# S5's recurrence by fours of tokens instead of pairs, in the first mixer of a two-block model on one Trainium2 core

## The chip, the cores and the metric

One core of one Trainium2 chip runs the kernel. The metric is device time in microseconds (us) of one execution, the median of several runs. A group of rows of the profile is one profiled execution of the same kernel.

## The reference

Two layers of a first block and two of a second run over one sequence of 256 tokens with 1024 channels, in 32-bit floats. Only the mixer of the first layer bears on the change. Half of its projected columns go through RWKV-7, the other half through S5, and a projection back follows:

```python
def s5_ssm(u, lam_re, lam_im, log_dt, b_re, b_im, c_re, c_im, d_skip, w_glu, b_glu):
    ug = u.reshape(b, t, 32, 16)                       # 32 groups of 16 channels
    lam = lax.complex(lam_re, lam_im)                  # 64 states a group
    lam_bar = jnp.exp(lam * jnp.exp(log_dt)[:, None])
    b_bar = ((lam_bar - 1.0) / lam)[..., None] * lax.complex(b_re, b_im)
    bu = jnp.einsum('gpi,btgi->btgp', b_bar, ug)
    # x[t] = lam_bar x[t - 1] + bu[t], an associative scan over the tokens
    y = jnp.real(jnp.einsum('gip,btgp->btgi', c_mat, states)) + d_skip * ug
    y = gelu(y.reshape(b, t, 512))
    return y * sigmoid(y @ w_glu + b_glu)
```

The mixer is `concat(rwkv7(z[..., :1824]), s5_ssm(z[..., 1824:])) @ hy_w_out` with `z = rms_norm(h) @ hy_w_in`, added to h. The layer's next part, attention to a memory of 256 rows, projects `rms_norm(mem)` to keys and values; that work doesn't depend on the mixer.

## The kernel before

Tokens lie along the free dimension and channels on the partitions. Every weight is loaded in tiles of 2048 columns (`weight`, L157) and split into two parts whose products are exact, wh by ScalarE (L177) and wl by VectorE (L180); a product by a weight is three matmuls (`mm3`). The order of the program is the order of priority. A planner puts each engine's instructions into one fixed queue by it, so an instruction that waits holds all behind it on its engine. A tile name with one buffer is handed to its next user, in program order, only when all readers of the tile before are done; the tiles named rw_... belong to RWKV's working memory and are lent to other work in this way. PSUM has four banks acc, two banks ps, and one each for s5_p and s5_py.

`hybrid_mix` (L898) puts the first mixer together. The projections (`hybrid_in`, L390) come first; u, the input of S5, is the last of them, two transposed banks copied by ScalarE. `next(ssm)` runs S5's setup before that. `mem_norm` (L973) loads the two blocks of the memory on SP's queue into rw_XK (one buffer, so the second block waits for the first's readers) and the gain into rw_MB. Then `mix` steps through `rwkv` (L426), which does two halves of 128 tokens with some 39 yields each, and between its yields takes steps of two others at written-out positions: the last projections and S5 in one chain, and `mem_kv`, the memory's projections to keys and values.

```python
at = (2, 5, 7, 9, 13, 20, 27, 34, 41, 45, 55, 61, 64, 75, 77), (21, 28, 35, 39, 49, 56, 65, 73, 76)
kv = mix(self.rwkv(z, y), (chain(proj, ssm), at[0]), (self.within_aside(self.mem_kv(0, mn, "")), at[1]))
```

RWKV bounces its small blocks through DRAM on SP's queue, and uses rw_MB (L538), rw_XK (L540), rw_G (L634) among others in each half. Its result of a half is split into yh and yl (L220).

S5 (`s5`, L718) holds 128 states on the partitions, two groups of channels at once, 16 such pairs (q). It carries the state from an odd token to the next: x[t] = l^2 x[t-2] + l B u[t-1] + B u[t], with the complex state turned back by its own angle so that the scan is real. The setup makes the decay and the angle (also once per input channel), Lt = l B (L784 to L791), the output matrices Cc and CL, and K0 = C B, the direct part of an even token, by 32 products of 32 columns. The loop has two halves j0 of four steps i; a step handles two q of 128 states by 128 pairs of tokens. It computes angles for them (L825 to L828), sine and cosine on ScalarE (`sincos`, L890), the state inputs (8 products of 32 rows, 128 columns), the turn (L839 to L842), four scans of 128 columns (L846), the turn back (L847 on), and the outputs: CL's and Cc's products of 128 columns on 32 output partitions, with the two q beside each other on the array, and K0's. After each half `d u` is added; a Gelu (L867) closes. `s5_glu` (L869) and the product by hy_w_out follow RWKV's end, then the residual (L302).

Of the kernel before, what the change touches and what calls it, by code (L numbers as in the profile page):

```python
# [19 lines left out]
S = 256  # L20
# [62 lines left out]
class Rows:  # L83
    """tiles that hold the 128-row blocks of a matrix, indexed [partitions, block, columns]"""
# [8 lines left out]
class Model:  # L93
# [23 lines left out]
    def phase(self, name, nb=2, nacc=4, nps=0, nx=1):  # L117
        """working memory of one phase"""
# [8 lines left out]
    def weights(self, name, nw, nraw):  # L127
        """buffers of the weights"""
# [6 lines left out]
    def more_raw(self, name, n):  # L135
        """n more buffers of the weights as loaded"""
# [20 lines left out]
    def weight(self, src, a, b, then=None):  # L157
        """src: AP [128, a, b] in DRAM -> (h, l) viewed [128, a, b], in halves of a; then() comes after the first half"""
# [27 lines left out]
    def fetch(self, src, a, b, pool=None):  # L186
        """src as loaded"""
# [5 lines left out]
    def wcols(self, w, c0, c1):  # L193
        """columns c0:c1 of w [K, N], all of K"""
# [3 lines left out]
    def wrows(self, w, k0, k1):  # L198
        """128-row blocks k0:k1 of w [K, N], all of N"""
# [16 lines left out]
    def split(self, h, l, src, scale=None):  # L216
        """src (F32) -> h + l; scale: [P, 1]"""
# [5 lines left out]
    def ntile(self, sh, name, bufs=2, dt=F32, pool=None):  # L223
        """a tile for the norms, which outlives the phases unless it belongs to work on the side"""
# [4 lines left out]
    def rstd(self, ss, n, width, eps, pool=None):  # L229
        """[128, n] sums of squares -> (ss / width + eps) ** -0.5"""  # L230
# [7 lines left out]
    def bcast(self, src, n, queue=None):  # L238
        """row src [n] of DRAM to all partitions"""
# [21 lines left out]
    def row_norm(self, src, g, xn):  # L261
        """a generator: xn = rms_norm of a block times g; returns the last instructions"""
# [8 lines left out]
    def norm_t(self, h, gain, parts=None, pre=None, tg=None):  # L271
        """rms_norm(h) * gain (or pre, its two token blocks), transposed and split: (xh, xl) [128, 8, 256]; parts: split by token too"""
# [29 lines left out]
    def residual(self, h, accs, hold=False):  # L302
        """h += accs (token block, column half)"""
# [45 lines left out]
    def rows_all(self, accs, w, at, order):  # L349
        """accs = at x w, in the order of the row blocks given"""  # L350
# [5 lines left out]
    def lin_t(self, w, c0, x):  # L356
        """256 columns of x @ w, transposed: bank [128, 2, 256] (column block, token)"""
# [25 lines left out]
    def shifted(self, p, f, i, dst, n=128):  # L383
        """token shift of the transposed projection p[:, f]: z + (z[t - 1] - z) * mu"""
# [5 lines left out]
    def hybrid_in(self, h, pool):  # L390
        """a generator: the projections in order of need; then yields for those of the last two"""
# [9 lines left out]
        # a small weight, in room of its own  # L401
# [19 lines left out]
        for j in range(2):  # L421
            p = self.lin_t(w, 1824 + j * 256, x)
            nc.scalar.copy(u[:, 2 * j:2 * j + 2, :], p.rearrange("p (f t) -> p f t", f=2))
            yield

    def rwkv(self, z, ya):  # L426
        """time mix of the shifted projections, a generator; split, transposed result into ya"""
# [25 lines left out]
        def head_sums(x):  # L453
            """sums over the channels of each head of x [128, 4, 128]: bank [:, :8], token on the partitions"""
# [5 lines left out]
        for hf in range(2):  # L460
# [4 lines left out]
            # normalised key  # L465
# [15 lines left out]
            # log decay, in-context learning rate  # L481
# [15 lines left out]
            # decay products from the start of each chunk of 64  # L497
# [9 lines left out]
            # alpha | rho, beta, kappa  # L507
# [12 lines left out]
            # products within chunks: rows s, columns t of alpha | rho  # L520
# [21 lines left out]
            # inverses of the 16 x 16 diagonal blocks, one block per partition  # L542
# [8 lines left out]
            tmp = T("Lt", [64, 64])  # L551
            Dm = DE[:, 0]
            with self.tc.issue_after(self.floor[1].ins):
                nc.vector.tensor_copy(Dm, self.cc("i16")[:64].rearrange("p (t s) -> p t s", t=16))
# [9 lines left out]
            Dc = T("Dc", [128, 2, 8, 16])  # L564
# [10 lines left out]
            # token-major copies  # L575
# [10 lines left out]
            # bonus weights  # L586
# [7 lines left out]
            # gate  # L594
# [8 lines left out]
            def both(lhsT, rhs):  # L603
                """block-diagonal lhsT: both chunks of each head at once"""
# [5 lines left out]
            def pairs(cols, lhsT, rhs):  # L610
                """[64 x 64] products for each head and chunk, chunk on the partitions"""
# [61 lines left out]
            # over the chunks  # L673
# [21 lines left out]
            # norm over each head, bonus, gate  # L695
# [22 lines left out]
    def s5(self, u, pool, brief, ps, yg):  # L718
        """the state is carried from one odd token to the next: x[t] = l^2 x[t - 2] + l B u[t - 1] + B u[t];
        an even token's output is C l x[t - 1] + C B u[t]"""  # L720
        nc, t = self.nc, self.t
        T = lambda name, sh, bufs=1: pool.tile(sh, F32, name="s5_" + name, bufs=bufs)
        V = nc.vector
        H = S // 2
        # per state (its index on the partitions | its group's input on them): decay, angle per token in turns
        N = 272
        par = self.work.tile([128, 1024], F32, name="rw_G", bufs=1)
        nc.scalar.dma_start(par[:, :3 * N], t["s5_par"])
        lr, li, dt = (par[:, e * N:(e + 1) * N] for e in range(3))
        tmp = self.work.tile([128, 1024], F32, name="rw_RW", bufs=1)  # L730
        r, f = tmp[:, :N], tmp[:, N:2 * N]
        m1, m2, q1, q2 = (tmp[:, 2 * N + e * 16:2 * N + (e + 1) * 16] for e in range(4))
        sico = self.work.tile([128, 1024], F32, name="rw_AR", bufs=1)[:, :2 * N].rearrange("p (e n) -> p e n", e=2)
        si, co = sico[:, 0], sico[:, 1]
        keep = T("keep", [128, 3, 16])
        fh, fl, r2 = (keep[:, e] for e in range(3))
# [8 lines left out]
        V.tensor_scalar(fh, f[:, :16], 1536.0, -1536.0, ALU.add, ALU.add)  # L745
        V.tensor_sub(fl, f[:, :16], fh)
        V.tensor_mul(r2, r[:, :16], r[:, :16])
        self.sincos(f, sico, N)
        V.tensor_mul(co, co, r)
        V.tensor_mul(si, si, r)  # L750
        # input coefficient
        a = slice(0, 16)
        lr, li = lr[:, a], li[:, a]
        cm = dt[:, a]
        V.tensor_scalar_add(cm, co[:, a], -1.0)
# [5 lines left out]
        V.tensor_mul(m2, si[:, a], li)  # L761
        V.tensor_add(q1, q1, m2)
        V.tensor_mul(q1, q1, m1)
        V.tensor_mul(q2, si[:, a], lr)
# [3 lines left out]
        # input and output matrices, block-diagonal over pairs of groups  # L768
        C = [T(n, [128, 16, 32], 2) for n in ("w1", "w2")]
        Bs = [self.work.tile([128, 16, 32], F32, name="rw_" + n, bufs=1) for n in ("Kt", "V")]  # L770
        for x, n in zip(C + Bs, ("s5_cT_re", "s5_cT_im", "s5_b_re", "s5_b_im")):
            nc.gpsimd.memset(x, 0.0)
            src = (t[n][0] if n in ("s5_b_re", "s5_b_im") else t[n]).rearrange("(q g) p i -> g p q i", g=2)
            for g in range(2):
                nc.scalar.dma_start(x[g * 64:(g + 1) * 64, :, g * 16:(g + 1) * 16], src[g])
        Bt, Lt = (brief.tile([128, 4, 2, 64], F32, name=n) for n in ("Bt", "Lt"))
        for e, n in enumerate(("re", "im")):
            nc.scalar.dma_start(Bt[:, :, e], t["s5_bT_" + n].rearrange("(j g) i p -> (g i) j p", g=8))

        def times(dst, x, y, cr, ci, sg):  # L780
# [1217 lines left out]
```

## Time and profile before

| | before |
|---|---|
| runs (us) | 2490.81, 2493.50, 2493.89; median 2493.5 |
| span of the profiled execution (us) | 2491.7 |
| its time outside the span | the page gives none |
| TensorE (PE) busy | 2406.4 us, 97% |
| VectorE (DVE) busy | 1863.9 us, 75% |
| ScalarE (ACT) busy | 1542.0 us, 62% |
| GpSimd (POOL) busy | 63.3 us, 3% |

PE is TensorE's matmul, PEld its load of weights. A row of instructions gives the line of the kernel, the engine, the operation, output<-inputs, the tile's shape and the number of instructions (x). In a timeline the first column is the start and the second the duration in us, both from the span's start; what stands in brackets is idle time before the instruction and what ended it. A 4-byte matmul leaves two records, one for each of its passes, but for the types that the split weights have. The granted clock is a share of 2.4 GHz; 0.5 is the lower level, 1.2 GHz. The busy shares are of the whole program; of the part that the change touches only the first mixer's stretches tell.

### The profile page before, as it was taken

To read this page: it belongs to the slowest core of one execution; us is meant where nothing else is said; L and a number is where in the kernel's file an instruction comes from. 1 tells how busy PE (TensorE), PEld (TensorE's weight loads), DVE (VectorE), ACT (ScalarE), POOL (GpSimd) and SP (SyncE) were. 2 spreads that over 40 slices of the span, in tenths; PEclk is the share of its full clock that TensorE was granted. 3 is DMA by queue.
4 is the path that set the end of the run, shared out by engine and by line. 5 is a ranking of instruction groups with operands and counts; after the bars stand their busy time and mean duration, and the time that the engine had idled before them with its cause. 6 is when DMAs were issued, how large, how long until landed. Compare 5 with 4: busy or idle time off the path is not lost. (4 is left out here: it accounts for less than half of the span.)

```text
span 2491.7 us, 37696 instructions
## 1 busy us (share of the span) xinstructions
PE 2406.4 (97%) x14914; PEld 2093.2 (84%) x14914; DVE 1863.9 (75%) x2533; ACT 1542.0 (62%) x2235; POOL 63.3 (3%) x78
## 2 busy tenths in 40 slices
PE   7999999999998999999999999999889999999998
PEld 7888789989887888888888888888778899887998
DVE  7888655556655989898989898989756776665776
ACT  5545554445544877777777777777655555555554
POOL 1000000001100000000000000000000000000000
PEclk9899999999999999999999999999989999998999
DMA  8323555554474989999999999999663455633653
GB/s 241 89 87 126 180 170 186 187 175 138 148 277 149 332 326 345 345 361 363 351 346 362 367 365 340 358 363 352 234 207 113 156 186 186 195 112 102 209 186 106
DMA packets 338764, 586.75 MB, mean 235 GB/s; under 512 B 28620, under 2 KB 173938, under 8 KB 338322
## 3 DMA queue, kind: packets, MB, share of 16 engines
q1 hardware_dynamic: 314752, 557.75, 64.6%
q10 hardware_dynamic: 23826, 26.50, 3.4%
q8 instruction: 119, 1.95, 0.3%
q14 instruction: 67, 0.55, 0.1%
HBM read 578.56 MB, written 6.82 MB: 235 GB/s over the span
## 5 line engine op out<-in xcount | busy, mean ns | idle before, releaser
L180 DVE TENSOR_TENSOR wl<-wraw,wh 128x1024 fp32r<-128x1024 f32 x1054 | 1247.1, 1221 | 349.7 <-ACT wh L177 345.2
L177 ACT CAST wh<-wraw 128x1024 fp32r<-128x1024 f32 x1054 | 1077.5, 1052 | 423.3 <-PE ps L203 254.3
L203 PE MATMUL ps<-wh,xh 128*128 128x512 f32 (+1 forms) x1472 | 458.8, 359 | 1.6 <-DVE xl L220 1.6
L203 PE MATMUL ps<-wl,xh 128*128 128x512 f32 (+1 forms) x1472 | 449.0, 352 | 0.0
L203 PE MATMUL ps<-wh,xl 128*128 128x512 f32 (+1 forms) x1472 | 448.8, 352 | 0.0
L203 PEld LDWEIGHTS ps<-wh,xh 128*128 128x128 f32 x1472 | 252.7, 193 | 40.1 <-issue 2.9
L203 PEld LDWEIGHTS ps<-wh,xl 128*128 128x128 f32 x1472 | 250.7, 192 | 38.8 <-issue 0.7
L203 PEld LDWEIGHTS ps<-wl,xh 128*128 128x128 f32 x1472 | 251.4, 192 | 36.2 <-issue 0.5
L203 PE MATMUL ps<-xh,wh 128*128 128x256 f32 x1424 | 208.2, 286 | 4.4 <-ACT wh L177 1.6
L203 PE MATMUL ps<-xh,wl 128*128 128x256 f32 x1424 | 207.0, 285 | 0.0
L203 PE MATMUL ps<-xl,wh 128*128 128x256 f32 x1424 | 206.0, 284 | 0.0
L203 PEld LDWEIGHTS ps<-xh,wh 128*128 128x128 f32 x1424 | 188.4, 192 | 10.7 <-issue 2.4
L203 PEld LDWEIGHTS ps<-xh,wl 128*128 128x128 f32 x1424 | 186.9, 192 | 1.6 <-issue 1.2
L203 PEld LDWEIGHTS ps<-xl,wh 128*128 128x128 f32 x1424 | 186.5, 192 | 1.2 <-issue 1.2
L203 PE MATMUL acc<-wh,e_ah 128*128 128x512 f32 x448 | 177.1, 395 | 0.1
L203 PE MATMUL acc<-wh,e_al 128*128 128x512 f32 x448 | 175.7, 392 | 0.0
L203 PE MATMUL acc<-wl,e_ah 128*128 128x512 f32 x448 | 175.6, 392 | 0.0
L203 PE MATMUL acc<-wh,ah 128*128 128x512 f32 x264 | 103.3, 391 | 0.0
L203 PE MATMUL acc<-wh,al 128*128 128x512 f32 x264 | 103.3, 392 | 0.0
L203 PE MATMUL acc<-wl,ah 128*128 128x512 f32 x264 | 103.2, 391 | 0.0
L203 PEld LDWEIGHTS acc<-wh,e_al 128*128 128x128 f32 x448 | 83.9, 187 | 20.3 <-DVE e_al L220 0.4
L203 PEld LDWEIGHTS acc<-wh,e_ah 128*128 128x128 f32 x448 | 84.1, 188 | 18.4 <-ACT e_ah L220 0.3
(582 smaller groups left out, 2795.3 us busy)
## 6 DMA issues: line engine op xcount, KB each, us to landing
wraw<-moe_w_up SPq DMA_DIRECT2D x112, 1024.0 KB, 7.3
wraw<-moe_w_gate SPq DMA_DIRECT2D x112, 1024.0 KB, 7.2
wraw<-moe_w_down SPq DMA_DIRECT2D x112, 1024.0 KB, 7.0
wraw<-w_up SPq DMA_DIRECT2D x44, 1024.0 KB, 5.1
wraw<-w_down SPq DMA_DIRECT2D x22, 1024.0 KB, 4.9
wraw<-w_in SPq DMA_DIRECT2D x20, 1024.0 KB, 6.4
wraw<-xa_w_kv SPq DMA_DIRECT2D x16, 1024.0 KB, 5.8
wraw<-da_w_qkv SPq DMA_DIRECT2D x12, 1024.0 KB, 5.1
```

The costliest lines, as they stand in the source:

```text
L177: nc.scalar.copy(h[:, :m], r)
L180: nc.vector.tensor_sub(l[:, :m], r, h.bitcast(F32)[:, :m])
L203: self.nc.tensor.matmul(out, lhsT, rhs, start=start, stop=stop)
```

## The change

S5 carries its state from one fourth token to the next.

- u is copied as [v, m], token 4 m + v, so that each of the four tokens of a four is a block of 64 columns.
- Parameters: 16 columns each in place of 272 (s5_par from 408 to 24 KB); the copy of B by input channel (0.26 MB) and the constants for it are gone, and the constants of the mixer are 448 columns narrower, or 0.23 MB.
- Setup: B l^k and C l^k for k = 0 to 3 come from one chain of seven complex products on VectorE, six operations of 256 columns each. The powers of B lie in rw_XK and rw_RW, those of C in a tile named y, which is RWKV's result later. All angles, 16 x 64, are made at once in rw_MB and rw_MT, and their sines and cosines kept in two tiles of 1024 columns.
- For each i of four, ScalarE spreads the powers into block-diagonal matrices BX (rw_De1) and LX by 4 and 2 copies; 8 products of 128 columns make K, the direct parts by distance 0 to 3; 8 transposes, in two acc banks, make the state input matrices B, copied out by ScalarE.
- The inputs of a four are stacked on the partitions in U (rw_G) by 16 transfers on ScalarE's queue, 32 partitions each.
- Loop: four steps of four q, each 128 states by 4 x 64 columns. The state inputs are 8 products of 128 rows and 64 columns; the scans two of 256 columns, whose decay row R4 GpSimd makes, with zeros where a q begins; the outputs 64 products of 64 columns, with neighbours on four different quarters of the output partitions. The direct terms are 4 products each of 192, 128, 64 columns with K, and of 64 with the skip d on the diagonal. The result of a step replaces its part of U.
- Channels are permuted by that; s5_w_glu, s5_b_glu and hy_w_out are permuted to match on the host, outside the timed kernel, and s5_glu restores the tokens' order as it splits.
- RWKV's unit matrix is made by two fills on GpSimd in place of a copy; two of its small tiles take names of others.
- S5 stands in `mix` by itself, at earlier positions.

```diff
-                nc.scalar.copy(u[:, 2 * j:2 * j + 2, :], p.rearrange("p (f t) -> p f t", f=2))
+            for f in range(2):
+                nc.scalar.copy(u[:, 2 * j + f].rearrange("p (v m) -> p v m", v=4), p[:, f * 256:(f + 1) * 256].rearrange("p (m v) -> p v m", v=4))
...
-            tmp = T("Lt", [64, 64])
+            tmp = T("Lp", [64, 64])
...
-                nc.vector.tensor_copy(Dm, self.cc("i16")[:64].rearrange("p (t s) -> p t s", t=16))
+            nc.gpsimd.memset(Dm, 0.0)
+            nc.gpsimd.memset(Dm.rearrange("p t s -> p (t s)")[:, ::17], 1.0)
...
-            Dc = T("Dc", [128, 2, 8, 16])
+            Dc = T("Lc", [128, 2, 8, 16])
...
+        def times(E, dst, x, y, cr, ci, sg, name):
+            for d, z, w, sub in ((dst[0], x, y, sg > 0), (dst[1], y, x, sg < 0)):
+                c = T(name, [128] + list(x.shape[1:]))
+                E.tensor_tensor(d, z, cr, ALU.mult)
+                E.tensor_tensor(c, w, ci, ALU.mult)
+                E.tensor_tensor(d, d, c, ALU.subtract if sub else ALU.add)
+        BC = [W(n, [128, 4, 16, 16]) for n in ("XK", "RW")]
+        C = [T(n, [128, 16, 16]) for n in ("w1", "w2")]
...
+        LC = pool.tile([128, 2, 4, 16, 16], F32, name="y")
+        times(V, (LC[:, 0, 0], LC[:, 1, 0]), C[0], C[1], b16(q1), b16(q2), 1, "R4")
+        V.tensor_scalar_mul(LC[:, 1, 0], LC[:, 1, 0], -1.0)
+        for k in range(3):
+            times(V, (BC[0][:, k + 1], BC[1][:, k + 1]), BC[0][:, k], BC[1][:, k], b16(ck), b16(sk), 1, "R4")
+            times(V, (LC[:, 0, k + 1], LC[:, 1, k + 1]), LC[:, 0, k], LC[:, 1, k], b16(ck), b16(sk), -1, "R4")
+        LX, BX = brief.tile([128, 4, 2, 4, 32], F32, name="LX"), W("De1", [128, 4, 2, 4, 32])
...
+        sc = self.gp.tile([128, 16 * M], F32, name="gain"), T("sc", [128, 16 * M])
+        y, z = W("MB", [128, 16, M]), W("MT", [128, 16, M])
...
+        self.sincos(y.rearrange("p q m -> p (q m)"), sc)
...
+        for i in range(4):
+            spread(BX, BC, i)
+            spread(LX, LC, i)
+            for j in range(4):
+                for e in range(2):
+                    self.mm(p[32 * i:32 * i + 32, j * 128:(j + 1) * 128], BX[:, j, e, 0, :], LX[:, j, e].rearrange("p d o -> p (d o)"),
+                            e == 0, e == 1)
+            for x in range(2):
+                pt = self.accs(1)[0]
+                for j in range(2):
+                    for e in range(2):
+                        nc.tensor.transpose(pt[:, (2 * j + e) * 128:(2 * j + e + 1) * 128], BX[:, 2 * x + j, e].rearrange("p k o -> p (k o)"), self.ident)
+                nc.scalar.copy(B[:, i, 2 * x:2 * x + 2], pt.rearrange("p (j e n) -> p j e n", j=2, e=2))
...
+            yield
+        U = W("G", [128, 4, 4, M])
+        for i in range(4):
+            for v in range(4):
+                nc.scalar.dma_start(U[32 * (3 - v):32 * (3 - v) + 32, i], u[32 * i:32 * i + 32, :, v * M:(v + 1) * M])
...
+        for i in range(5):
+            if i:
+                h = i - 1
...
+                for v in range(4):
+                    for n, (cx, x) in enumerate(terms):
+                        for j in range(4):
+                            c = (h + j) % 4
+                            o = py[32 * c:32 * c + 32, v]
+                            if v < 3:
+                                self.mm(o[:, 1:], LX[:, j, cx, v + 1, :], x[:, j, :-1], False, False)
+                            else:
+                                self.mm(o, LX[:, j, cx, 0, :], x[:, j], False, n == 3)
+                nc.scalar.copy(U[:, h], py)
...
+            spread(LX, LC, i)
...
+            R4 = T("R4", [128, 4, M])
+            G.tensor_tensor(R4, self.cc("reset")[:, None, :M].to_broadcast([128, 4, M]), r4[:, i::4, None].to_broadcast([128, 4, M]), ALU.mult)
...
+        nc.scalar.activation(yg, U.rearrange("p i v m -> p i (v m)"), AF.Gelu_apprx_tanh)
...
-            at = (2, 5, 7, 9, 13, 20, 27, 34, 41, 45, 55, 61, 64, 75, 77), (21, 28, 35, 39, 49, 56, 65, 73, 76)
-            kv = mix(self.rwkv(z, y), (chain(proj, ssm), at[0]), (self.within_aside(self.mem_kv(0, mn, "")), at[1]))
+            at = (2, 5, 7, 9), (4, 6, 8, 10, 12, 16, 20, 24, 28), (21, 28, 35, 39, 49, 56, 65, 73, 76)
+            kv = mix(self.rwkv(z, y), (proj, at[0]), (ssm, at[1]), (self.within_aside(self.mem_kv(0, mn, "")), at[2]))
```

## Rows read from the trace of the kernel before

**Rows 1.** The page of the kernel before, its first line.
```profile
span 2491.7 us, 37696 instructions
```

**Rows 2.** Windows: stretch, length, busy PE PEld DVE ACT POOL, clock, DMA share, GB/s.
```profile
45.00:85.00 40.00, 36.99 (x394) 35.11 (x395) 37.39 (x77) 28.77 (x48) 2.08 (x1) 1.00 0.57 156
85.00:118.00 33.00, 31.26 (x237) 25.42 (x232) 24.36 (x73) 12.15 (x23) 1.10 (x2) 0.74 0.21 58
118.00:232.00 114.00, 111.86 (x1204) 100.66 (x1204) 98.70 (x244) 58.44 (x103) 6.23 (x6) 1.00 0.30 92
232.00:264.30 32.30, 29.47 (x376) 25.89 (x376) 21.45 (x37) 12.64 (x23) 1.64 (x1) 1.00 0.55 190
```

**Rows 3.** Windows, the stretch from 90 to 107 alone.
```profile
90.00:107.00 17.00, 16.50 (x86) 13.40 (x86) 13.88 (x42) 4.24 (x10) 0.55 (x1) 0.51 0.31 96
```

**Rows 4.** Timeline of PE, one step of the S5 loop, 173 to 181.
```profile
173.08 2.08 PE L203 MATMUL s_p<-zu,s_B 32*128 32x128 f32 x16
175.09 0.39 PE L203 MATMUL ps<-wl,xh 128*128 128x256 f32 x1
...
177.68 1.06 PE L203 MATMUL s_py<-s_w,CL 128*32 128x127 f32 x16
178.57 1.04 PE L203 MATMUL s_py<-s_w,Cc 128*32 128x128 f32 x16
179.54 1.06 PE L203 MATMUL acc<-call,rw_sq 128*128 128x8 f32 x8
180.53 0.42 PE L203 MATMUL s_py<-zu,s_K 32*32 32x128 f32 x4
```

**Rows 5.** Timeline of PE, RWKV's sums of 8 columns and K0's product, 57 to 62.
```profile
57.55 0.95 PE L203 MATMUL acc<-call,rw_sq 128*128 128x8 f32 x8
58.35 0.36 PE L203 MATMUL ps<-xh,wl 128*128 128x256 f32 x1
...
60.67 0.22 PE L203 MATMUL s_p<-Cc,rw_V 128*32 128x32 f32 x1
...
61.43 0.39 PE L203 MATMUL ps<-xh,wl 128*128 128x256 f32 x1
```

**Rows 6.** Timeline of PE, two rows of four transposes, and what follows, 201 to 203.
```profile
201.83 0.66 PE L583 MATMUL acc<-ident,zv 128*128 128x128 f32 x4
...
202.85 0.38 PE L203 MATMUL s_p<-zu,s_B 32*128 32x128 f32 x1
```

**Rows 7.** Groups of VectorE by form, 16 to 278: count | busy us, mean ns | idle.
```profile
L180 DVE TENSOR_TENSOR wl<-wraw,wh 128x1024 fp32r<-128x1024 f32 x44 | 53.3, 1221 | 5.6 <-ACT wh L177 5.6
L846 DVE TENSOR_TENSOR_SCAN s_st<-s_keep,s_w 128x128 f32<-128x128 f32 x32 | 11.6, 404 | 0.0
...
L847 DVE TENSOR_TENSOR s_w<-s_st,s_sc 128x512 f32<-128x512 f32 x8 | 5.5, 684 | 0.0
...
L840 DVE TENSOR_TENSOR s_w<-s_w,s_w 128x256 f32<-128x256 f32 x8 | 3.3, 416 | 0.0
```

**Rows 8.** Timelines of ACT and DVE, places where memory is handed on, 65 to 265.
```profile
65.26 0.68 DVE L791 TENSOR_TENSOR CL<-CL,s_st 128x512 f32<-128x512 f32 x1
...
83.54 0.63 ACT L253 ACTIVATE xl<-rw_XK 128x512 fp32r<-128x512 f32 x1 [1.82 <-PE ps L203]
...
98.20 0.74 DVE L538 TENSOR_TENSOR rw_MB<-acc,call 128x256 f32<-128x256 f32 x2
...
112.80 1.29 DVE L540 TENSOR_TENSOR rw_XK<-acc,call 128x512 f32<-128x512 f32 x2 [4.69 <-PE ps L290]
...
133.79 0.68 DVE L634 TENSOR_TENSOR rw_G<-rw_RW,acc 128x512 f32<-128x512 f32 x1
...
264.50 0.68 DVE L220 TENSOR_TENSOR yl<-rw_ka,yh 128x512 fp32r<-128x512 f32 x1
```

**Rows 9.** Timelines of POOL and of ACT's DMA queue.
```profile
59.38 2.08 POOL L473 TENSOR_TENSOR rw_ks<-rw_ks,mhalf 128x8 f32<-128x8 f32 x1 [42.48 <-DVE rw_ks L472]
...
133.91 0.37 ACTq L996 DMA_DIRECT2D kv<-a_m_kT  x1
```

More of the change, by code (lines that the diff above doesn't have):

```diff
@@ L721, in s5 @@
         nc, t = self.nc, self.t
[L722 to L728, printed above, removed]
-        lr, li, dt = (par[:, e * N:(e + 1) * N] for e in range(3))
[L730 to L736, printed above, removed]
+        T = lambda name, sh: pool.tile(sh, F32, name="s5_" + name)
+        W = lambda name, sh: self.work.tile(sh, F32, name="rw_" + name, bufs=1)
+        V, G = nc.vector, nc.gpsimd
+        M = S // 4
+        N = 16
+        par, tmp = W("G", [128, 3 * N]), W("AR", [128, 6 * N])
+        nc.scalar.dma_start(par, t["s5_par"])
+        lr, li, dt = (par[:, e * N:(e + 1) * N] for e in range(3))
+        r, f, si, co, m1, m2 = (tmp[:, e * N:(e + 1) * N] for e in range(6))
+        keep = T("keep", [128, 7, 16])
+        fh, fl, r4, q1, q2, ck, sk = (keep[:, e] for e in range(7))
         nc.scalar.activation(dt, dt, AF.Exp)
@@ L760, in s5 @@
         V.tensor_mul(q1, cm, lr)
-        V.tensor_mul(m2, si[:, a], li)
+        V.tensor_mul(m2, sk, li)
         V.tensor_add(q1, q1, m2)
         V.tensor_mul(q1, q1, m1)
-        V.tensor_mul(q2, si[:, a], lr)
+        V.tensor_mul(q2, sk, lr)
         V.tensor_mul(m2, cm, li)
@@ L767, in s5 @@
         V.tensor_mul(q2, q2, m1)
[L769 to L775, printed above, removed]
@@ new lines, in s5 @@
+        skip = T("skip", [128, 4, 32])
+        for i in range(4):
+            g = slice(32 * i, 32 * i + 32)
+            V.tensor_tensor(skip[g], self.ident[g, None, g].to_broadcast([32, 4, 32]),
+                            self.pps("s5_d", 4)[g, :, None].to_broadcast([32, 4, 32]), ALU.mult)
+        yield
+        self.sincos(y.rearrange("p q m -> p (q m)"), sc)
+        K = T("K", [128, 4, 4, 32])
+        p = ps.tile([128, 512], F32, name="s5_p")
+        B = brief.tile([128, 4, 4, 2, 128], F32, name="B")
@@ new lines, in s5 @@
+        LC = LC.rearrange("p e k q o -> p (e k) q o")
+        for i in range(4):
[5 more added lines that the diff above has]
+                            e == 0, e == 1)
+            for x in range(2):
+                pt = self.accs(1)[0]
+                for j in range(2):
+                    for e in range(2):
+                        nc.tensor.transpose(pt[:, (2 * j + e) * 128:(2 * j + e + 1) * 128], BX[:, 2 * x + j, e].rearrange("p k o -> p (k o)"), self.ident)
+                nc.scalar.copy(B[:, i, 2 * x:2 * x + 2], pt.rearrange("p (j e n) -> p j e n", j=2, e=2))
+            if i == 3:
+                nc.scalar.copy(K, p.rearrange("p (j d o) -> p j d o", j=4, d=4))
+                V.tensor_tensor(K[:, :, 0], K[:, :, 0], skip, ALU.add)
+            yield
@@ L881, in s5_glu @@
                              (ygh[:, k, :], ygl[:, k, :]), k == 0, k == 3)
-            sg = pool.tile([128, 2, S], F32, name="s5_st")
+            sg = pool.tile([128, 2, S], F32, name="s5_K")
             for f in range(2):
@@ L904, in hybrid_mix @@
             self.alias = {"xn": "rw_XK", "xn1": "rw_MT"}
-            y = [pool.tile([128, 4, S], F32R, name="y" + e) for e in "hl"]
             proj = self.hybrid_in(h, pool)
@@ L915, in hybrid_mix @@
                 next(ssm)
+            y = pool.tile([128, 2, 4, S], F32R, name="y")
+            y = [y[:, 0], y[:, 1]]
             self.alias = {"xn": "rw_XK", "xn1": "rw_MT", "gain": "rw_MB"}
@@ L1864, in layouts @@
     src = {k: cols(a[k]) for k, _ in PP if k in a}
+    i, c, r = np.ogrid[:4, :4, :32]
+    order = (128 * ((c - i) % 4) + 32 * i + r).ravel()
+    src["s5_b_glu"] = cols(np.asarray(a["s5_b_glu"]).ravel()[order])
     src["da_q_gain"], src["da_k_gain"] = (cols(np.tile(np.asarray(a[k])[0], 2)) for k in ("da_q_gain", "da_k_gain"))
@@ L1868, in layouts @@
         assert src[k].shape[1] == w, k
-    for k in ("s5_b_re", "s5_b_im", "s5_c_re", "s5_c_im"):
+    out["s5_w_glu"] = np.ascontiguousarray(np.asarray(a["s5_w_glu"])[:, order][:, :, order])
+    rows = np.concatenate([np.arange(512), 512 + order])
+    out["hy_w_out"] = np.ascontiguousarray(np.asarray(a["hy_w_out"])[:, rows])
+    for k in ("s5_c_re", "s5_c_im"):
         out[k[:4] + "T" + k[4:]] = np.ascontiguousarray(np.asarray(a[k])[0].transpose(0, 2, 1))
     per = [np.asarray(a[k])[0] for k in ("s5_lam_re", "s5_lam_im")] + [np.repeat(np.asarray(a["s5_log_dt"])[0][:, None], 64, 1)]
-    rows = lambda v: np.repeat(v.reshape(4, 8, 64).transpose(1, 0, 2).reshape(8, 256), 16, 0)
-    out["s5_par"] = np.ascontiguousarray(np.concatenate([e for v in per for e in (cols(v), rows(v))], 1))
+    out["s5_par"] = np.ascontiguousarray(np.concatenate([cols(v) for v in per], 1))
     w, bf = np.asarray(a["w_in_2"]), np.asarray(a["b_f_2"])
@@ L1907, in const_tiles @@
     c["i64"] = s == q
-    c["i16"] = np.tile(np.eye(16).reshape(1, 256), (128, 1))
     c["reset"] = np.tile(np.arange(128) % 64 != 0, (128, 1))
     c["mpi4"] = np.full((128, 1), -math.pi / 4)
-    c["time"] = np.tile(2 * np.arange(128), (128, 1))
+    c["time"] = np.tile(4 * np.arange(64), (128, 1))
     return c
```

172 lines of the change are left out of this document (71 added, 101 removed).

## The prediction, made before the changed kernel ran

> **What bounds the kernel now.** I read the page for the span, then a table of the first mixer by stretches, then TensorE's order of time in one S5 step, then VectorE's groups, last the places where one tile's memory passes from one user to the next. The change touches only the first mixer, whose last stretch in the table ends at 264.3 [rows 2] of 2491.7 us [rows 1] and is followed by its closing products; everything behind it shifts with its end. In that mixer TensorE is the busy engine: 36.99 of 40 us while the projections run (45 to 85), 31.26 of 33 (85 to 118), 111.86 of 114 (118 to 232), 29.47 of 32.3 (232 to 264.3) [rows 2]. VectorE is nearly as full in the first of these (37.39 of 40) and has air in the others. So the end moves with TensorE's work plus what TensorE loses. Its losses lie in one place: from 85 to 118 it stands 1.74 us, and from 90 to 107 the granted clock is 0.51 [rows 3], the lower level of 1.2 GHz, which doubles what runs there: 17 us for 8.5 us of work. Together 10.2 us. The drop came after short products of 32 rows, transposes and a wait.
>
> **TensorE's part.** One step of the old loop (eight of them) costs: state inputs 175.09 - 173.08 = 2.01 us, outputs 0.89 and 0.97, direct term 0.42 [rows 4], 4.3 us in all, 34.3 for eight. The product for K0 needs 61.43 - 60.67 = 0.76 us for 62 of its 64 records [rows 5], say 0.9. Old sum 35.2 us. A 4-byte product is two records.
> New loop, four steps. State outputs: 64 products of 64 columns, 128 records, neighbours on four different groups of 32 output columns. With 32 columns the K0 records, which rotate over the four groups too, start every 0.76/62 = 12.3 ns [rows 5], 49 ns within a group; with 128 columns and two groups taking turns they start every 0.97/16 = 61 ns [rows 4], 121 ns within a group. A third of the way between gives 73 ns for 64 columns, or 18.3 ns a record over four groups: 2.34 us. Ends: 12.3 ns (the 32-column row) and 36.6 ns (only two groups side by side). Direct terms: per group 192, 128, 64 and 64 columns, 169 + 121 + 73 + 73 = 436 ns a record, 0.87 us. State inputs: 16 records of 64 columns on all 128 rows, between 0.80/8 = 0.10 us (8 columns) [rows 5] and 2.01/16 = 0.126 us (128 columns) [rows 4]; I take 0.11: 1.76 us. A step is 4.97 us, four 19.9.
> New setup: 64 records of 128 columns that stay in one group at 0.121 us make 7.75; 32 transposes at (202.85 - 201.83)/8 = 0.1275 us (two rows of four) [rows 6] make 4.1. New sum 31.7, so the change removes 3.5 us (ends: 7 removed, 7 added).
> The rows show records starting 12.3 ns apart on average. The Trainium skill, TensorE: Matmul & The Clock Gate, "Wait — 56ns, not 53.3ns?", says that start to start never falls below about 25 ns however few the columns. By that the 512 output records would take 12.8 us, not 9.4, and the sum would be no gain at all; the trace speaks against it.
>
> **VectorE's part.** Old loop: three operations of 512 columns (0.684), four of 256 (0.416), four scans of 128 (0.404) [rows 7] and eight angle operations of 128 columns (0.28, on the line through 0.684 and 0.416): 7.6 us, 61 for eight. New: three of 512, four of 256, two scans of 256 (between 0.54, the elementwise slope, and 0.81, double; I take 0.67): 5.1 us, 20 for four. In the setup the old matrices took some 12 operations of 512 and 10 of 256, 12.4 us; the chain of powers is seven calls of six operations of 256, 42 x 0.416 = 17.5 us, the angles of all groups four operations at 1.22 [rows 7] and one cheaper, 5.6. So the setup grows by some 11 us in the stretch where VectorE has 2.6 us free, and the loop shrinks by 41 where TensorE hardly waits. The first delays, the second is mostly hidden: I count 0 for it (2 us gain at most, the share of TensorE's 2.1 idle us from 118 to 232 that VectorE could cause).
>
> **Copies, transfers, POOL.** Each of the four setup groups needs six copies on ACT before its products and two after them, at most 0.63 us each (512 columns, the row at 83.54 [rows 8]); 3.8 + 1.94 + 1.02 = 6.8 us a group, since one buffer each of BX and LX makes the next group wait for the products and the transposes. ACT is busy 12.15 of 33 us from 85 to 118 [rows 2], so its time is free, the latency is not. The 16 transfers stand on ACT's queue behind the copies of u, 0.37 us an issue [rows 9]: 5.9 us, during which the later copies and weight splits of ACT wait; four suffice for the first step. They fall into the same ACT gap: 0 (6 us if ACT were full). The decay row on POOL costs between 0.416 us (VectorE, 256 columns) [rows 7] and 2.08 (POOL's power) [rows 9] a step; it is ready while VectorE forms w1 and w2 (about 3 us): 0, and at most 8. The GPSIMD Engine Reference of the Trainium skill, section 3.1, gives an elementwise operation there about twice VectorE's time, 0.8 us as an estimate; no run here shows it. The smaller constants and parameters take about 0.9 MB off the first 45 us; TensorE is busy there anyway: 0. The zero fills on POOL are early: 0.
>
> **What is late next.** The powers lie in rw_XK and rw_RW, the angles in rw_MB and rw_MT. Program order gives rw_XK first to them, then to the two memory blocks, then to RWKV's XK. Now the statistics of the first memory block start at 83.54, as soon as the projections end, MB is written at 98.20 and XK at 112.80, after a wait for the last transposes of the memory [rows 8]. After the change the memory's load waits on SP's queue until the fourth group has read the powers; behind it stand RWKV's bounces through DRAM and the weights of the memory projections. The old matrices are done at 65.26 + 0.68 [rows 8], the new chain some 11 us later, near 76, if it runs as the old did; groups take 6.8 us, so the last read is near 76 + 3 x 6.8 + 2 = 98 and XK would come some 20 us after that with the old spacing shortened, near 118. MB comes near 116, and the four acc banks of RWKV are held till then. So from 85 to 118 TensorE has about three setup groups (8.9), one and a half steps (7.5) and 16 transposes (2.0): 18.4 us, some 3 more of RWKV. It stands 12 us, in place of the 10.2 now lost. That is 1.8 us against the 3.5.
> Sum: -3.5 + 1.8 = -1.7 us, of a span of 2491.7. The page gives no time around the span; the runs' median is 1.8 above it. On the median: 2491.8.
>
> **The rivals.** *The hole closes* (faster): if the setup groups run under the projections, or the clock stays up, the 8.5 us come back with the 3.5: 12 less, 2481.5. For it: ACT has 11 us free between 45 and 85, and the new products use all rows of the array. Against: nothing of the setup can start before a VectorE chain in the fullest stretch.
> *rw_G is held* (slower): the stacked inputs U stand in rw_G until the Gelu has read them, and RWKV's G, first written at 133.79 [rows 8], needs that place. With the setup ending near 103 and each step at 5.1 (VectorE) + 2.3 (TensorE) + about 2.1 for hand-overs, S5 ends near 141, with its Gelu 144: 10 us late. RWKV's second half must follow, and its last result at 264.50 [rows 8] starts the closing products. It decides once the lateness exceeds what the second half, free of S5, makes up. TensorE cannot fill the tail then: 10 late, 2 made up, 8 more, 2501.5 (between 5 and 13 more). For it: from 232 on TensorE already waits most, 2.83 of 32.3 us [rows 2]. Against: four old S5 steps (30 us of VectorE) leave the second half.
> *The products don't run four abreast*: at 36.6 ns a record the outputs cost 9.4 us more, 2501. The rows of 32 columns speak against it; I give it 0.04, within slower.
>
> **How the numbers follow.** A measurement of this kernel can tell about 0.2%, 5 us, from no change. No measurable change: 0.38, the losses trade places. Faster: 0.34. Slower: 0.28 (rw_G 0.24). The time is that of the likeliest case, whose own range is 2488.5 to 2498.5. The range for all reaches to the middles of the other two and their bounds: 2479 to 2505.
>
> **What would show it.** Right: S5's TensorE records near 32 us, outputs about 18 ns apart; VectorE's S5 work about 30 us less; the memory's first statistics near 100; XK near 118; TensorE idle for some 10 us between 85 and 118; first G near 144 and the last yl still near 264. Wrong: XK before 113 or a granted clock of 1.00 throughout (then faster); yl later than 270 (then slower); output records at 25 ns or more.

## The result, and the profile after

The changed kernel took 2507.4 us, median of 7 runs (2504.7 to 2519.7), against 2493.5: a ratio of 1.0063 (95% interval 1.0043 to 1.0084): slower, and above the range of 2479 to 2505. The first lines of its page:

```profile
span 2505.7 us, 38305 instructions
...
PEclk9899899999999999999999999999989999999999
```

The windows of the same four stretches as [rows 2], same columns:

```profile
45.00:85.00 40.00, 38.39 (x301) 36.36 (x300) 35.71 (x79) 33.29 (x58) 2.43 (x2) 0.96 0.37 119
85.00:118.00 33.00, 27.46 (x265) 24.31 (x269) 15.97 (x43) 14.64 (x33) 2.88 (x4) 0.73 0.32 87
118.00:232.00 114.00, 109.07 (x1581) 100.00 (x1574) 80.97 (x165) 53.93 (x96) 11.33 (x10) 0.97 0.35 111
232.00:264.30 32.30, 29.92 (x365) 26.36 (x364) 19.78 (x30) 13.27 (x19) 0.00 (x0) 1.00 0.37 114
```

The hole from 85 to 118 came out about as forecast: TensorE stands 5.5 us and the clock is 0.73. New is the stretch behind it: 4.9 us idle where 2.1 were and a clock of 0.97 for 1.00, with VectorE at 81 of 114 us for 98.7. TensorE has less to do and still ends later. The places where memory is handed on, timelines of ScalarE and VectorE, to be set beside [rows 8]:

```profile
97.79 0.64 ACT L253 ACTIVATE xl<-rw_XK 128x512 fp32r<-128x512 f32 x1
...
114.65 0.74 DVE L539 TENSOR_TENSOR rw_MB<-acc,call 128x256 f32<-128x256 f32 x2
...
126.09 1.28 DVE L541 TENSOR_TENSOR rw_XK<-acc,call 128x512 f32<-128x512 f32 x2
...
157.15 0.69 DVE L635 TENSOR_TENSOR rw_G<-rw_RW,acc 128x512 f32<-128x512 f32 x1 [6.13 <-ACT wh L177]
...
191.95 0.69 DVE L468 TENSOR_TENSOR rw_kk<-zk,ppt 128x512 f32<-128x512 f32 x1
...
278.94 0.68 DVE L220 TENSOR_TENSOR y<-rw_ka,y 128x512 fp32r<-128x512 f32 x1
```

XK is 13.3 us later than before, G 23.4, the last y 14.4; the span is 14.0 longer. The fifth row is where RWKV's second half of tokens begins (its first product on VectorE, at 177.39 in the kernel before), the sixth its last y. Cut there, the windows of the kernel before are

```profile
16.00:177.40 161.40, 153.63 (x1504) 141.28 (x1505) 136.56 (x326) 85.94 (x152) 8.61 (x9) 0.95 0.46 130
177.40:264.50 87.10, 83.66 (x912) 73.38 (x911) 68.39 (x152) 45.17 (x71) 3.32 (x2) 1.00 0.39 129
```

and those of the changed kernel

```profile
16.00:192.00 176.00, 163.74 (x1992) 152.14 (x1993) 129.14 (x274) 100.19 (x183) 15.05 (x16) 0.93 0.42 124
192.00:279.00 87.00, 76.89 (x768) 68.15 (x767) 58.44 (x114) 41.13 (x65) 5.12 (x3) 0.97 0.38 124
```

This is the view that the prediction lacked. The second half takes 87 us in both, with TensorE full in one (83.7 of 87.1) and not in the other (76.9). The first grew by 14.6. Taking half of what ran at the lower clock as loss, and the rest as work at full clock, TensorE's first half holds 153.8 us of work for 145.6, 12.3 us idle for 7.8, and 10.0 us lost to the clock for 8.1: 8.2 + 4.5 + 1.9 = 14.6. In the second half the work fell by 8.7 us (75.0 for 83.7), and idle time and clock took its place (12.0 us for 3.4). Over the whole program TensorE's work fell by 6.4 us (2364.3 for 2370.6), it stood 12.6 us longer (97.8 for 85.2), and the lower clock cost 7.8 us more (43.6 for 35.8): together the 14.0 us of the span. S5's old half steps had ended near 220, inside RWKV's second half; the new ones end near 153, inside the first.

### The profile page after: what moved, and what is told of

Read it like the earlier page. It is cut to its first block, busy times and chain, and to the rows that moved or that the text cites. A ratio compares the mean times of both kernels' runs of the same rounds, so it can differ in the third digit from the quotient of the medians.

```text
span 2505.7 us, 38305 instructions
## 1 busy us (share of the span) xinstructions
PE 2407.8 (96%) x15234; PEld 2096.7 (84%) x15234; DVE 1842.9 (74%) x2438; ACT 1548.7 (62%) x2255; POOL 69.0 (3%) x84
## 5 line engine op out<-in xcount | busy, mean ns | idle before, releaser
L203 PEld LDWEIGHTS ps<-wl,xh 128*128 128x128 f32 x1472 | 253.2, 193 | 35.8
```

The source lines that it names most:

```text
L203: self.nc.tensor.matmul(out, lhsT, rhs, start=start, stop=stop)
```

## The experiments

Each group of runs has its own runs of the kernel before beside it, with medians between 2490.9 and 2494.3 us. The ratios are to these, and times of different groups are compared by their ratios.

**Which tile holds RWKV back?** The prediction's slower rival was that U keeps rw_G from RWKV. Making room for U takes some scratch and one small tile elsewhere, so there is a control.

```diff
-            times(V, (BC[0][:, k + 1], BC[1][:, k + 1]), BC[0][:, k], BC[1][:, k], b16(ck), b16(sk), 1, "R4")
+            times(V, (BC[0][:, k + 1], BC[1][:, k + 1]), BC[0][:, k], BC[1][:, k], b16(ck), b16(sk), 1, "K")
...
-            R4 = T("R4", [128, 4, M])
+            R4 = B[:, max(i - 1, 0), 0].rearrange("p e n -> p (e n)").rearrange("p (j m) -> p j m", j=4)
```


> Control. The changed kernel with four kilobytes of room made and not used: the chain of powers takes its scratch from K's tile, the decay row R4 lies in the part of B that the step before has read, one output of the gate lies in zv's tile, the memory's gain has one buffer. U is still in rw_G. Every theory: the changed kernel's time, 2507 us, within 4 us; first G of RWKV near 157.


```diff
-        U = W("G", [128, 4, 4, M])
+        U = brief.tile([128, 4, 4, M], F32, name="U")
```


> The control with U in a tile of its own, so that rw_G is free from the start of the mixer. Theory H (RWKV's first half is late because it waits for S5 to leave rw_G, and its second half then has no work beside it): first G before 146 in place of 157.15, the last y of the second half some 8 to 14 us earlier than 278.94, time 2494 to 2499. Rival F (S5's early place in the order is at fault: its steps go before RWKV's on every engine and nothing is left beside the second half; the tile is hidden): first G stays near 155, or comes earlier without the end, time 2504 to 2510. Rival D (ScalarE's queue stands 13 us behind the 16 transfers): no change, 2504 to 2510.


```diff
-            self.alias = {"xn": "rw_XK", "xn1": "rw_MT", "gain": "rw_MB"}
+            self.alias = {"xn": "rw_MT", "gain": "rw_MB"}
```


> The changed kernel with the memory's two blocks loaded into rw_MT in place of rw_XK, so that they wait neither for the powers of B nor hold RWKV's XK. Theory H: XK near 100 in place of 126.09, but G still waits for the Gelu near 153, so the time moves little, 2500 to 2508. Rival X (the hand-on of rw_XK, the step that the prediction priced at 1.8 us, carries the loss): first G near 140, time 2490 to 2497. Rivals F and D: 2504 to 2510.

The fourth run has both edits.

> U in a tile of its own and the memory's blocks in rw_MT. Theory H: both hand-ons gone, first G near 135, so that of the loss only the clock and the setup's place stay and the 6.2 us of TensorE's work show: 2485 to 2495. Rivals F and D: 2504 to 2510, with 13 us of idle TensorE between 175 and 290.

Measured: 2511.9, 2512.1, 2506.7 and 2511.5 us, ratios to before 1.0070, 1.0068, 1.0058, 1.0071, each interval within 1.0040 and 1.0086. Theory H falls: with U in its own tile the time is that of its control, and G's first write came at 161.6, after the control's 157.9. Rival X falls too, since XK came at 100.1 in the third run as expected and the time stayed. In the last run XK was written at 100.1 and rw_G was free, yet ScalarE's, TensorE's and VectorE's timelines read

```profile
144.14 1.18 ACT L627 COPY rw_MT<-acc 64x512 f32<-64x512 f32 x2 [0.40 <-PE acc L203]
```
```profile
148.28 1.64 PE L203 MATMUL s_py<-s_w,LX 128*32 128x63 f32 x104
...
152.46 0.65 PE L203 MATMUL ps<-wh,xl 128*128 128x256 f32 x4
...
153.38 1.95 PE L203 MATMUL acc<-rw_RW,rw_MT 128*128 128x128 f32 x16
```
```profile
154.91 0.68 DVE L635 TENSOR_TENSOR rw_G<-rw_RW,acc 128x512 f32<-128x512 f32 x1
```

MT stands ahead of G: it came 15.7 us later than in the kernel before (128.42). The products that read it, and whose result G takes, ran at 153.38, behind S5's last outputs and one of the memory's projections (143.98 to 152.46), and TensorE is full there. The tile was a wait that another had already covered. The times alone would say less, since the clock moves them: in this run the second half begins at 189.3 for the changed kernel's 192.0 but takes 91.0 us for 87.0, with 6.5 us lost at the lower clock for 1.9. What ScalarE's transfers cost (rival D) these runs don't separate.

**Is it the place of S5's work?** Three runs move only positions, the third in the kernel before, whose tiles and instructions stay.

```diff
-            at = (2, 5, 7, 9), (4, 6, 8, 10, 12, 16, 20, 24, 28), (21, 28, 35, 39, 49, 56, 65, 73, 76)
+            at = (2, 5, 7, 9), (4, 6, 8, 10, 16, 24, 31, 38, 45), (21, 28, 35, 39, 49, 56, 65, 73, 76)
```


> The kernel with U in its own tile and the memory in rw_MT, and S5's loop steps moved later among RWKV's: 16, 24, 31, 38, 45 in place of 12, 16, 20, 24, 28 (the last spread must stay ahead of RWKV's first result, at 39). Theory F (S5's steps ahead of RWKV's products, which stand at 25 to 29, hold its first half back by their latency, and leave nothing beside its second): RWKV's MT before 138 in place of 144, first G before 146, time 2490 to 2500. Rival P (the setup ahead of the loop is at fault: it takes TensorE and ScalarE from the projections, whose end comes 8 us later, and from RWKV's first products, LD at 91.3 for 78.3): 2505 to 2513, MT still near 144 or later.


```diff
+            at = (2, 5, 7, 9), (6, 10, 14, 18, 22, 27, 32, 38, 45), (21, 28, 35, 39, 49, 56, 65, 73, 76)
```


> The same with the setup spread too: 6, 10, 14, 18 in place of 4, 6, 8, 10, and the loop at 22, 27, 32, 38, 45. Theory F: as the run before, 2490 to 2500. Rival P: better than the run before by 4 us or more, LD near 85, 2498 to 2506.


```diff
-            at = (2, 5, 7, 9, 13, 20, 27, 34, 41, 45, 55, 61, 64, 75, 77), (21, 28, 35, 39, 49, 56, 65, 73, 76)
+            at = (2, 5, 7, 9, 12, 14, 16, 18, 20, 22, 25, 28, 64, 75, 77), (21, 28, 35, 39, 49, 56, 65, 73, 76)
```


> The kernel before with nothing changed but the positions of S5's eight old half steps: 12 to 28, as early as the changed kernel has its own, in place of 13 to 61. Theory F: RWKV's first G moves from 133.8 to 145 or later, the second half stands alone, 2501 to 2512. Rival P: within 4 us of the kernel before, 2489 to 2497.

Measured: 2513.2 (1.0077), 2513.0 (1.0079), and 2514.6 (1.0075, interval 1.0058 to 1.0092). The old S5, placed early, loses as much as the change does, and more than expected. Its windows, cut where its second half starts:

```profile
16.00:195.30 179.30, 167.19 (x1670) 152.78 (x1671) 152.05 (x367) 90.61 (x161) 8.27 (x9) 0.93 0.40 114
195.30:284.30 89.00, 79.48 (x769) 70.63 (x768) 57.94 (x115) 40.22 (x65) 5.00 (x3) 0.93 0.42 134
```

So the place alone is enough to lose that much. The first two runs contradict theory F as it was worded, though: RWKV's MT came at 136.3 and 129.8 and G at 144.4 and 141.8, as it said, but the second half began at 199.4 and 196.2, no earlier. Rival P falls as well: in the second run RWKV's first LD came at 81.2 for 91.7 in the first, and no time was gained. Getting RWKV's products ahead within the half did nothing. The reading, argued here and put to the test below, is that S5's last spread must stand before RWKV's first result (both use the tile y), so that nearly all of S5's work is still in that half. The theory was changed to two bounds (T): up to the second half each microsecond of TensorE's work counts, behind it RWKV's own chain sets the time.

**Moving other work out of the first half.** The memory's projections are some 5.8 us each.

```diff
-            at = (2, 5, 7, 9), (4, 6, 8, 10, 12, 16, 20, 24, 28), (21, 28, 35, 39, 49, 56, 65, 73, 76)
+            at = (2, 5, 7, 9), (4, 6, 8, 10, 12, 16, 20, 24, 28), (21, 41, 45, 49, 54, 59, 64, 69, 74)
```


> The changed kernel with nothing moved but the steps of the memory's projections: 21, 41, 45, 49, 54, 59, 64, 69, 74 in place of 21, 28, 35, 39, 49, 56, 65, 73, 76, so that three of the eight projections, some 17 us of TensorE's work, leave RWKV's first half. Theory T (two bounds: up to the start of RWKV's second half, at 192.0 for 177.4, TensorE is full and the end of that stretch moves with all work put into it, 153.8 us at full clock for 145.6; the second half takes RWKV's own chain 87 us with or without work beside it, so work is free there): the second half starts near 180 and still takes 87 us, 2491 to 2500. Rival Q (the order of the queues inside the first half delays RWKV, not the sum of the work): second half's start stays at 188 or later, 2503 to 2510.

> The same positions of the memory with U in its own tile and the memory's blocks in rw_MT. Theory T: with the hand-ons gone too the first half can follow its work, start of the second at 172 to 180, 2484 to 2496. Rival Q: as the run with both hand-ons gone, 2503 to 2511.

> The run before with S5's steps at 6, 10, 14, 18, 22, 26, 29, 33, 37. Theory T: the same work in the same half, so within 4 us of the run before. Rival Q: better than the run before by 5 us or more, as RWKV's products go ahead of S5's.

> The kernel before with the memory's steps moved as in the other three. Theory T: its second half is full already (83.6 us of work and 3.4 us lost in 87), so the work only changes places: the second half grows beyond 87 us by about what the first loses, 2489 to 2500. Rival Q: within 3 us of before too, and the second half's length stays at 87.

Measured: 2515.1 (1.0100), 2511.6 (1.0084), 2511.3 (1.0078), 2497.1 (1.0021, interval 1.0009 to 1.0033). Half of T came true: the second half began at 184.1, 180.7 and 180.0. It took 90 to 93 us for the 87 expected, so that the last y came at 274.2, 273.5 and 271.2, some 5 to 8 us earlier than in the changed kernel. In the kernel before the second half began at 162.9 and grew to 104.1 us, as it has no room: TensorE is busy 100.45 of 104.10.

```profile
162.90:267.00 104.10, 100.45 (x987) 88.62 (x985) 77.30 (x172) 52.24 (x86) 7.00 (x4) 0.95 0.45 144
```

But no time came of it in the new kernels: the first two lie above both theories' ranges, and the third within 4 us of the second, as T says. The windows of the second of these runs, the last one reaching to the end of the closing products:

```profile
180.70:273.50 92.80, 79.36 (x812) 74.12 (x812) 57.54 (x115) 41.07 (x70) 8.06 (x4) 0.89 0.38 121
273.50:295.20 21.70, 21.70 (x93) 17.42 (x92) 9.58 (x12) 7.50 (x11) 0.56 (x1) 0.97 0.47 174
```

The closing takes 21.7 us after the last y, against 8.4 in the changed kernel (278.94 to 287.4): the gate's and the output's weights stand behind the memory's on SP's queue, where the last of hy_w_out left at 264.8 for 238.0, and their products ran after RWKV in place of beside it. Work can be hidden in the second half only if its weights are there in time.

**S5 over both halves.** The changed kernel cannot place S5 as the old one did, since the powers of C lie in RWKV's result tile until the last step. Here RWKV's two results get a tile each, and U's later parts and S5's results lie in parts of B that are already used; the control has all that at the old positions.

```diff
-            y = pool.tile([128, 2, 4, S], F32R, name="y")
+            y = [pool.tile([128, 2, 4, 128], F32R, name=n) for n in ("y0", "y")]
-        U = W("G", [128, 4, 4, M])
+        U = [U0] + [part(B[:, 0, c]) for c in range(3)]
+        res = [U0] + [part(B[:, 1, c]) for c in range(3)]
```


> Control of the two runs after it: U's parts in U0 and in B, RWKV's two results in two tiles of their own, the memory's blocks in rw_MT, S5's positions as in the changed kernel (4 to 28). Every theory: as the run with both hand-ons gone, 2505 to 2513, second half's start near 190.


```diff
-            at = (2, 5, 7, 9), (4, 6, 8, 10, 12, 16, 20, 24, 28), (21, 28, 35, 39, 49, 56, 65, 73, 76)
+            at = (2, 5, 7, 9), (4, 6, 8, 10, 13, 27, 41, 52, 61), (21, 28, 35, 39, 49, 56, 65, 73, 76)
```


> The control with S5's loop steps at 13, 27, 41, 52, 61, over both halves as the kernel before has its own (13 to 61), which the changed kernel's tiles did not allow. Theory T (the loss comes from S5's steps having moved out of RWKV's second half, which takes 87 us by its own chain, into the first, where each us counts): second half's start at 172 to 182, time 2488 to 2498, that is 12 us or more below the control. Rival Q (the order of the queues in the first half, which the setup spoils wherever the loop stands): 2503 to 2512. Rival S (the new steps are a longer chain of their own wherever they stand): 2500 or more, with the last y later than the second half's start by over 95 us.


```diff
+            at = (2, 5, 7, 9), (6, 10, 14, 18, 22, 34, 45, 55, 64), (21, 28, 35, 39, 49, 56, 65, 73, 76)
```


> The same with the setup spread to 6, 10, 14, 18 and the loop at 22, 34, 45, 55, 64. Theory T: 2484 to 2497, at or below the run before. Rival Q: lower than the run before by 5 us or more. Rival S: 2500 or more.

Measured: 2507.7 (1.0078), 2498.5 (1.0033, 1.0021 to 1.0044), 2496.3 (1.0024, 1.0011 to 1.0038). Same instructions, other positions: the second run is 9.2 us under the control, out of the 16.8 us by which the control stands above the kernel before (2490.9 in this group), and the windows show it where T puts it. The control, then the run over both halves:

```profile
16.00:189.30 173.30, 159.79 (x1991) 147.27 (x1992) 128.63 (x274) 99.90 (x183) 13.85 (x16) 0.96 0.44 126
189.30:277.50 88.20, 78.12 (x768) 69.47 (x767) 58.57 (x113) 41.13 (x65) 5.12 (x3) 0.96 0.39 123
```
```profile
16.00:182.20 166.20, 153.62 (x1673) 142.22 (x1674) 121.20 (x260) 95.45 (x178) 13.17 (x15) 0.94 0.43 125
182.20:269.00 86.80, 82.29 (x1073) 74.20 (x1073) 63.12 (x124) 43.94 (x68) 4.30 (x3) 0.98 0.42 137
```

The first half lost 7.1 us, the second took 4.2 us more of TensorE's time and became no longer. At full clock the work moved is 9.5 us less in the first half (145.5 for 155.0) and 5.9 us more in the second (80.6 for 74.7); 3.4 us more went to the lower clock in the first. The gain is less than the 12 us expected, and 2498.5 lies just above the range. In the third run one wait stands out on TensorE:

```profile
103.25 0.69 PE L302 MATMUL ps<-ident,rw_MT 128*128 128x128 f32 x2 [8.38 <-DVE rw_MT L1040]
```

The memory's second block can only be loaded once the first has left the one tile they share, and TensorE's fixed order waits for it.

**A version ahead of both.** The memory's blocks get rw_MT and rw_G (free, now that U is gone from it), with the positions of the third run, with others, and in the kernel before.

```diff
-            self.alias = {"xn": "rw_XK", "xn1": "rw_MT", "gain": "rw_MB"}
+            self.alias = {"xn": "rw_MT", "xn1": "rw_G", "gain": "rw_MB"}
-        pre = [self.ntile([128, D], "xn", self.nb) for _ in range(2)]
+        pre = [self.ntile([128, D], n, self.nb) for n in ("xn", "xn1")]
```


> The run with S5 over both halves (22 to 64) and the memory's two blocks in two tiles, rw_MT and rw_G, so that the second block's load no longer waits for the first one's transposes. In the run before, TensorE stood 8.4 us at 94.9 for that. Theory T with the hole: 5 to 9 us lower, 2487 to 2493, the same as the kernel before or under it. Rival Q (the hole is filled by other waits): within 3 us of the run before, 2494 to 2499.

> The same with other positions, setup 5, 8, 11, 15, loop 20, 34, 46, 56, 66. Theory T: as long as the loop lies over both halves the exact places matter little: within 4 us of the run before it. Rival Q: over 5 us off.

> The kernel before with the memory's two blocks in rw_MT and rw_G and nothing else: what the two tiles are worth without the new S5. If the hole at 88.9 with the lower clock behind it (1.4 us and 8.1 us) comes from the second block's late load: 2484 to 2489. If it comes from RWKV's short products and the end of the projections: within 3 us of before, 2489 to 2496.

Measured: 2484.0 (2479.1 to 2487.4), ratio 0.9958 with the interval 0.9942 to 0.9974; 2495.0 (0.9997); 2497.3 (1.0015). The first is faster than both kernels, and more than expected:

```profile
16.00:169.00 153.00, 143.18 (x1658) 133.80 (x1659) 120.40 (x257) 95.28 (x177) 12.79 (x15) 1.00 0.47 136
169.00:259.30 90.30, 85.24 (x1088) 76.98 (x1088) 62.76 (x126) 44.08 (x68) 4.40 (x3) 0.97 0.40 131
```

The hole closed, and with it the clock stayed at 1.00 through the first half, where the run before had lost 2.0 us to it. The second run is a miss: moving the setup and the loop's first step up by one to three places and three later steps down by one or two cost 11 us, with TensorE idle 3.4 us at 111.2 and the lower clock from 112.7 to 119.6; RWKV's second row of LD came at 91.0 for 85.9. So the places inside a half matter too, by as much as the move between the halves did; T doesn't explain that. The third shows that the two tiles alone give the old S5 nothing. With the same tiles the new S5, placed over both halves, is 13 us ahead of it (2484.0 against 2497.3) with one set of positions and 2 us ahead with the other (2495.0); for the old S5 one set was tried.

## Why the prediction was wrong

- **The step that failed** is in its first paragraph: "So the end moves with TensorE's work plus what TensorE loses." As a sum it holds, but the losses were looked for in one place, and work taken away was counted as an earlier end. Between 85 and 118 the losses grew by 2.5 us (1.8 forecast), everywhere else by 17.9. Up to RWKV's second half the sentence holds as a forecast too. Behind it TensorE's 83.66 of 87.10 us were work put beside a chain that takes its time anyway: in the runs that leave the memory's steps in place the second half took 85 to 92 us, with 72 to 86 us of work. Where TensorE had room, its length went with the lower clock rather than with the work: 87.0 us with 1.9 us lost to the clock in the changed kernel, 91.0 with 6.5 in the run with both hand-ons gone, both with 74 to 75 us of work; 86.8 with 1.7 lost and 80.6 of work in the first run over both halves. In the kernel before the two bounds were nearly equal there, and a full engine was read as the bound.
- From that followed the wrong sign of a term. "Against: four old S5 steps (30 us of VectorE) leave the second half" stood as a reason against the slower rival. Leaving it was worth nothing (87.0 us for 87.1), and arriving in the first half cost 8.2 us more work at full clock, with 6.4 us more lost. The earlier positions in `mix` are part of the change, and the prediction's sum has no term for them. The control and the run over both halves put 9.2 us on the place; the rest of the loss is not shown piece by piece.
- **The rival of rw_G** had the late end (last y at 278.94; "later than 270" was its sign) but not the cause. G was 13 us later than even it said, and freeing the tile gave nothing. Its time of 2501.5 was the nearest of the cases, by luck: the side was right, the mechanism wrong.
- **The hand-on of rw_XK** went as forecast up to MB: first statistics at 97.79 (near 100), MB at 114.65 (116), and a hole of 12.3 us from 85 to 118 (12). XK came at 126.09, 8 us after the 118 forecast, and of the hole 5.5 us were idle time, where some 10 were named as a sign, and 6.8 the clock. It wasn't what decided: without that hand-on XK came at 100.1, and the time was 2506.7.
- **TensorE's sum** was nearly right. One step of the new loop, its order of time:

```profile
141.12 1.97 PE L203 MATMUL s_py<-s_w,LX 128*32 128x63 f32 x128
143.02 1.10 PE L203 MATMUL s_p<-rw_G,B 128*128 128x64 f32 x8
144.06 0.86 PE L203 MATMUL s_py<-zu,s_K 32*32 32x192 f32 x24
144.74 0.29 PE L203 MATMUL s_py<-zu,s_skip 32*32 32x64 f32 x8
144.96 1.10 PE L203 MATMUL s_p<-rw_G,B 128*128 128x64 f32 x8
```

  128 output records in 143.02 - 141.12 = 1.90 us are 14.8 ns each (18.3 forecast), the direct terms 0.90 us (0.87), the state inputs 0.13 us a record (0.11). Down to the last closing product the work at full clock fell from 240.7 to 234.3 us, 6.4 for 3.5 forecast and 7 at the good end; over the whole program it is 6.4 too. By the floor of 25 ns that the Trainium skill states (TensorE: Matmul & The Clock Gate, "Wait — 56ns, not 53.3ns?") the outputs would take 3.2 us a step, as an estimate; where neighbours lie on four groups of columns the measurement decides against it.
- **VectorE's** S5 lines went from 76.5 to 45.2 us of busy time, added up from the traces: 31.3 for 30 forecast. Over the whole program its busy time fell by 21.0 us (1863.9 to 1842.9), since records that follow each other closely overlap. **ScalarE's transfers** were under-priced; its queue and two of POOL's four decay rows:

```profile
97.28 0.75 ACTq L848 DMA_DIRECT2D rw_G<-zu  x1
...
99.42 6.41 ACTq L848 DMA_DIRECT2D rw_G<-zu  x6
...
110.37 3.82 ACTq L848 DMA_DIRECT2D rw_G<-zu  x5
```
```profile
128.63 2.86 POOL L887 TENSOR_TENSOR s_R<-call,s_keep 128x256 f32<-128x256 f32 x1 [4.68 <-DVE s_w L898]
...
137.60 1.06 POOL L887 TENSOR_TENSOR s_R<-call,s_keep 128x256 f32<-128x256 f32 x1 [6.11 <-DVE s_w L898]
```

  Sixteen took 13.5 us, 0.84 each for 0.37. No run isolates them. The control of the last-but-one group issues them by fours: RWKV's second half starts at 189.3 there and in the run with both hand-ons gone, and the ratios are 1.0078 and 1.0071. The two differ in tiles too, so this speaks against a large share and doesn't settle it. The decay rows took 0.61, 0.61, 2.86 and 1.06 us, where 2.08 was the bound; the estimate after the Trainium skill's GPSIMD Engine Reference, section 3.1, was 0.8, and the four lie on both sides of it. They were hidden: each ended 4 us or more before the scan that reads it (131.5 and 136.2 for the longest).
- **Left open:** how the 6.4 us of idle time and clock in the first half split between S5's setup, its loop and ScalarE's transfers, and why two neighbouring sets of positions differ by 11 us. The second must lie in the order of the queues, since nothing else differs; which wait makes it isn't shown.

## What to carry to other kernels

A full engine is the bound only where no chain beside it takes as long. Before pricing work that moves, cut the profile at the points where a dependent chain hands over (here the start of its second half), and compare, piece by piece, the chain's length with the engine's work: moving work from a piece that the chain sets into one that the engine sets can cost nearly its whole length, even where the sum of work falls. Tiles shared to save memory also fix where work may stand; that price can show in the order alone, and not as a wait.

## What the runs showed that was not expected

A change of positions alone, with every instruction the same, moved the time by some 20 us in the kernel before and by 11 us between two well-spread versions. And closing one wait of 8.4 us brought more than its length: 10.1 us of the profiled spans, 12.3 of the medians (2496.3 to 2484.0), and by the ratios, as the two runs lie in different groups, 1.0024 to 0.9958. Of the 10.1 us, 9.0 lie ahead of RWKV's second half, which itself took 3.2 us longer, and 4.4 behind the last y. The granted clock, at the lower level from 97.2 to 107.4 around that wait, stayed at 1.00 there, and so it did after it (264.5 to 300), where it had been 0.95. That the wait caused the second of these isn't shown.
